# Biased attention: the ones column of V set on GpSimd, and a planner that counts TensorE at half clock in the prologue

## The chip, the cores and the metric

The kernel runs on one core of a Trainium2 chip. The metric is the time of one execution on the device, in microseconds; the figure of a kernel is the median of several executions. The core has engines that run side by side, each with its own queue worked off in order: TensorE (PE, matrix products and transposes), VectorE (DVE), ScalarE (ACT, here the exponentials), GpSimd (POOL) and SyncE (SP). Loads and stores are DMAs that are issued from the queues of SP, ACT and POOL. Engines wait for each other by semaphores.

## The reference

```python
scale = 1.0 / np.sqrt(head_dim)
scores = scale * np.matmul(q, k.transpose(0, 1, 3, 2))
scores = scores + bias                      # one bias, 1024 x 1024, for all heads
scores_max = np.max(scores, axis=-1, keepdims=True)
attn = np.exp(scores - scores_max) / (np.sum(np.exp(scores - scores_max), axis=-1, keepdims=True) + 1e-8)
return np.matmul(attn, v).astype(np.float32)
```

q, k and v are float32 of 4 batches x 8 heads x 1024 x 64, so 32 heads, which the kernel takes as 16 pairs.

## The kernel before

**Arithmetic.** The kernel writes exp(scale*qk + bias) as exp(scale*qk) * exp(bias). The scores are kept transposed, keys on the partitions. One "bank" is 128 keys x 512 queries of one head; a pair has 32 banks (2 halves of the queries, 8 key chunks, 2 heads), and there are 512 in all. For each bank:

- TensorE forms kT by qT into PSUM (`s_fill`, L125). Three banks make one "slot"; two slots fit in PSUM. Slot g is called S g below; slots 0 and 1 hold one and two banks.
- ScalarE takes the exponential of a slot at once into bf16 tiles E (`s_exp`, L130).
- VectorE multiplies two banks at a time by the exponential of the transposed bias (`mul_pair`, L148).
- TensorE multiplies E by V, which has a 65th column of ones, so that the row sums come out with the product (`av_bank`, L160). After 8 key chunks VectorE takes the reciprocal of the sum (L170) and scales the result (L171) into an output tile; SP stores one head at a time (L174).

The bias is transposed once on TensorE (`b_fill`, L138) and exponentiated by ScalarE (`b_exp`, L143) into eb, in four tiles: (0,0), (0,4), (1,0), (1,4), the first number the half of the queries, the second the first of four key chunks. A multiply needs the tile of its half and chunk.

Q and K of a pair are transposed in four "pieces" (`transpose_pe`, L88): K and Q, each in two halves. Every piece goes through one of two PSUM buffers, xa and xb, and VectorE copies it out (K: a plain copy, L101; Q: a multiply with a mask that keeps the two heads apart, L97). The av products use the same two buffers, and give one back when it has been evacuated. When the second Q piece of a pair has been copied, GpSimd is told to load q and k of the pair after the next two and V of the pair after the next.

**The prologue** is written out by hand: SP and ACT load the first halves of Q and K of pair 0 as float32; VectorE clears and fills the constants (L183 to L200), among them the ones column of all of V, `vall[:, :, :, D:D1]`, 256 elements in each of 128 partitions, 65 elements apart; GpSimd makes the identity and then issues, in this order, kr and qr of pair 0 (second halves), the first half of the bias (btraw), V of pair 0 (two loads, L80), K and Q of pair 1 (L74, L75), the second half of the bias (L203), V of pair 1, K and Q of pair 2. The first V load has to come after the ones column. VectorE casts the two heads of Q to bf16 (L221), TensorE transposes them (L224), VectorE copies them out (L225), and the first two slots run.

**The planner** sets everything after that. From L239 on, Python simulates the engines while it emits the program: it keeps the times t_act, t_pe and t_dve in nanoseconds, and at each step emits what can start first: ScalarE's next exponential, VectorE's next item (copies and evacuations before multiplies), or what `pe_pick` chooses for TensorE. TensorE's choices are the next fill of a slot or of a bias tile (`pe_fill`), the next piece (`pe_piece`) and the next av bank (`pe_av`). A piece or av bank is taken only if it ends before a limit, which is set by when the next fill is ready and when it has to be done for ScalarE not to wait. The planner's costs are constants (L239 and L240: a bank's matmul 216, an av bank 170, a piece 350, an exponential 45 + 427 for each bank, a multiply 600); the clock starts at T0; and a few times are fixed: `bias_at` and `raw_at` say when the loads of the bias and of pairs 0, 1 and 2 are taken to have landed. These costs decide only the order of the instructions in each queue. On the chip, semaphores decide when they run.

Order of the fills from slot 2 on: S2, S3, S4, S5, S6, bias tile (0,0), S7, bias tile (0,4), S8, S9, S10, bias tile (1,0), S11, bias tile (1,4), S12, and then slots alone.

Of the kernel before, what the change touches and what calls it, by code (L numbers as in the profile page):

```python
# [15 lines left out]
def kernel(  # L16
# [15 lines left out]
    nc = tc.nc  # L32
    B, H, S, D = q.shape
    P = 128
    NCH = S // P
    D1 = D + 1
# [25 lines left out]
    vall = consts.tile([P, 2 * NP, NCH, D1], BF)  # L62
# [15 lines left out]
    def load_v(pr):  # L78
        for t in range(2):
            nc.gpsimd.dma_start(out=vall[:, 2 * pr + t, :, :D], in_=vf[pr, :, t])  # L80
# [38 lines left out]
    def s_fill(g):  # L119
        ps = ps_s.tile([P, 3, HQ], F32, tag="s", name="ps")  # L120
        open_ps[("S", g)] = ps
        for j, b in enumerate(slots[g]):
            pr, h, qh, kc = banks[b]
            qT, kT = trs[(pr, 0)], trs[(pr, 1)]
            nc.tensor.matmul(ps[:, j, :], kT[:, kc, :], qT[:, h, qh * HQ:(qh + 1) * HQ],  # L125
                             start=True, stop=True)
# [5 lines left out]
    def b_fill(qh, k0):  # L132

        ps = ps_s.tile([P, 3, 2 * HQ], BF, tag="s", name="pb").rearrange("p b (j q) -> p (b j) q", j=2)
        open_ps[("B", qh, k0)] = ps
        for j in range(4):
            for i in range(QC):
                nc.tensor.transpose(ps[:, j, i * P:(i + 1) * P],  # L138
                                    btraw[:, qh * QC + i, :].rearrange("p (kp kc) -> p kc kp", kc=NCH)[:, k0 + j, :],
                                    ident[:])  # L140
# [36 lines left out]
    with tc.manual_schedule():  # L177
# [18 lines left out]
        for t in range(2):  # L196
            nc.vector.memset(qT0[t * D:(t + 1) * D, 1 - t, :HQ], 0.0)
            for u in range(2):
                nc.vector.memset(mask[t * D:(t + 1) * D, u, :], 1.0 if t == u else 0.0)
        nc.vector.memset(vall[:, :, :, D:D1], 1.0)  # L200
        load_v(0)
        load_qk(1)
        nc.gpsimd.dma_start(out=btraw[:, QC:, :], in_=bf_[:, QC:, :])  # L203
# [35 lines left out]

        EXP, EXP0, QK, AV, TP = 427, 45, 216, 170, 350
        MUL, COPYQ, COPYK, EVAC, SEM = 600, 650, 420, 620, 80
        order = [("S", g) for g in range(2, NS)]
        for at, x in ((5, (0, 0)), (7, (0, 4)), (11, (1, 0)), (13, (1, 4))):
            order.insert(at, ("B",) + x)
        NO = len(order)
        T0 = 7500.0
        t_act, t_pe, t_dve = T0 + 700, T0, T0 + 500
        filled = []  # L250
        act_end = []
        x_free = {"xa": T0 + 500, "xb": T0}
        x_unit = {}
# [3 lines left out]
        for pr in range(1, NP):  # L257
            pieces += [(pr, 1, 0), (pr, 0, 0), (pr, 1, 1), (pr, 0, 1)]
        piece_end = {(0, 1, 0): T0, (0, 0, 0): T0}
        eb_at = {}  # L260
        exp_at = {0: T0, 1: T0 + 700, 2: T0 + 700}
        mul_at = {}
# [9 lines left out]
        def unit_of(b):  # L272
            return banks[b][:3]

        dve_q = []

        def cost_act(i):
            item = order[i]
            return EXP0 + EXP * (len(slots[item[1]]) if item[0] == "S" else 4)

        def act_end_of(i):
            if i < 0:
                return T0
            if i < len(act_end):
                return act_end[i]
            return max(t_act, filled[i] + SEM if i < len(filled) else 0) + sum(
                cost_act(j) for j in range(len(act_end), i + 1))

        def pe_fill():
            i = len(filled)  # L290
            if i >= NO or i - 2 >= len(act_end):
                return None
            ready = act_end_of(i - 2) + SEM
            item = order[i]
            if item[0] == "S":
                for b in slots[item[1]]:
                    pr, h, qh, kc = banks[b]
                    for key in ((pr, 1, kc // QC), (pr, 0, qh)):
                        if key not in piece_end:
                            return None  # L300
                        ready = max(ready, piece_end[key] + SEM)
                cost = QK * len(slots[item[1]])
            else:
                ready = max(ready, bias_at[item[1]])
                cost = 2 * TP + 250

            def emit(t):
                if item[0] == "S":
                    s_fill(item[1])
                else:  # L310
                    b_fill(item[1], item[2])
                filled.append(t + cost)
            return ready, cost, emit

        def pe_piece():
            if not pieces:
                return None
            pr, which, half = pieces[0]
            if pr not in raw_at or pr not in raws:
                return None  # L320
            i = min(len(filled), NO - 1)
            while order[i][0] != "S":
                i -= 1
            at = slots[order[i][1]][0]
            if at < (pr - 2) * 32 + 8:
                return None

            left = NCH - av_next % NCH
            busy = x_unit.get(unit_of(av_order[av_next])) if av_next % NCH else None
            tags = sorted((x_free[x], x) for x in x_free if x != busy)  # L330
            if busy and left < 4 and at < pr * 32 - 16:
                return None
            if not busy and av_next and at < pr * 32 - 16 and tags[0][0] + SEM < t_pe and len(tags) > 1 and tags[1][0] > t_pe:
                return None
            free, tag = tags[0]
            ready = max(free + SEM, raw_at[pr][1 - which])

            def emit(t):
                pieces.pop(0)
                copy = transpose_pe(pr, which, half, tag)  # L340
                cost = COPYK if which else COPYQ
                x_free[tag] = 1e12

                def run(t2):
                    copy()
                    x_free[tag] = t2 + cost
                    piece_end[(pr, which, half)] = t2 + cost
                    if which == 0 and half == 1:
                        if pr + 3 < NP:
                            load_qk(pr + 3)  # L350
                            raw_at[pr + 3] = (t2 + 7000, t2 + 7000)
                        if pr + 2 < NP:
                            load_v(pr + 2)
                dve_q.append((t + TP + SEM, 0, cost, run))
            return ready, TP, emit

        def pe_av():
# [23 lines left out]
                    dve_q.append((t + AV + SEM, 1, EVAC, run))  # L381
            return ready, AV, emit

        def pe_pick():
            f = pe_fill()
            best = None
            i = len(filled)
            if f and f[0] <= t_pe:
                return (max(t_pe, f[0]),) + f[1:]
            limit = 1e12  # L390
            if f:
                limit = max(f[0], act_end_of(i - 1) - f[1] - 100)
            elif i < NO:
                limit = max(act_end_of(i - 2) + SEM, act_end_of(i - 1) - 750)
            for c in (pe_piece(), pe_av()):
                if c is None:
                    continue
                start = max(t_pe, c[0])
                if start + c[1] > limit:
                    continue  # L400
                if best is None or start < best[0]:
                    best = (start,) + c[1:]
            if f and (best is None or f[0] <= best[0]):
                best = (max(t_pe, f[0]),) + f[1:]
            return best
# [19 lines left out]
        def act_pick():  # L425
            i = len(act_end)
            if i >= len(filled):
                return None
            return max(t_act, filled[i] + SEM), cost_act(i), i

        while len(act_end) < NO or av_next < NB or dve_q:
            c = []
            a, d, p = act_pick(), dve_pick(), pe_pick()
            if a:
                c.append((a[0], 0))
            if d:
                c.append((max(t_dve, d[0]), 1))
            if p:
                c.append((p[0], 2))
            t, who = min(c)  # L440
            if who == 0:
                i = a[2]
                item = order[i]
                t_act = t + a[1]
                act_end.append(t_act)
                if item[0] == "S":
                    s_exp(item[1])
                    for b in slots[item[1]]:
                        exp_at[b] = t_act
                else:  # L450
                    b_exp(item[1], item[2])
                    for kc in range(4):
                        eb_at[(item[1], item[2] + kc)] = t_act
            elif who == 1:
                if d in dve_q:
                    dve_q.remove(d)
                t_dve = t + d[2]
                d[3](t)
            else:
                t_pe = t + p[1]  # L460
                p[2](t)


# [28 lines left out]
```

## Time and profile before

| | us |
|---|---|
| median of 4 executions | 254.51 (254.13 to 254.57) |
| the profiled execution | 254.13 |
| its span | 252.4 |
| ScalarE busy | 239.0 (95%) |
| TensorE busy | 232.4 (92%) |
| VectorE busy | 226.0 (90%) |
| GpSimd busy | 52.6 (21%) |
| exponentials, L130 | 172 instructions, 230.1 |
| multiplies, L148 | 256 instructions, 163.5 |

The span reaches from the first to the last thing that the profiler saw; the execution's own time is 1.73 us longer. Lines of a timeline give start and duration in us, engine, line, operation, what is written and read, how often in a row, and in square brackets the idle time before and what ended it. Lines of the table of groups end with busy us, the mean ns of one, and the idle time of the engine before them. "ps" is the PSUM of the scores, "px" that of the pieces, "po" that of the av products. A score matmul of 512 columns takes 0.45 us of TensorE in the prologue (five from 7.24 us on in 2.24) and 0.27 later (three from 9.98 us on in 0.82).

### The profile page before, as it was taken

The page shows a single profiled execution, that of the slowest core. Times are in us where ns is not written, and L with a number is a line of the kernel's source. Part 1 is how long each engine was busy: PE and PEld are TensorE (multiplying, and loading weights), DVE is VectorE, ACT ScalarE, POOL GpSimd, SP SyncE. Part 2 cuts the span into 40 slices and gives each one's busy share as a digit, 9 for nine tenths or more (in the row PEclk, how much of TensorE's full clock was granted, in tenths as well). Part 3 has the DMA queues.
Part 4 walks back from the last instruction along what each step waited for, and adds up shares of the span by engine and source line. Part 5 has one row for each costly group of instructions (what it writes and reads, how often), then busy time and mean ns, then how long its engine had stood idle before and what let it go on. Part 6 is the DMA issues. An engine that isn't in the chain of part 4 may idle for free.

```text
span 252.4 us, 7265 instructions
## 1 busy us (share of the span) xinstructions
PE 232.4 (92%) x3142; PEld 141.3 (56%) x3142; DVE 226.0 (90%) x461; ACT 239.0 (95%) x180; POOL 52.6 (21%) x72
## 2 busy tenths in 40 slices
PE   6869999999999999999999999999999999999982
PEld 2346655565565566565555566565555655555651
DVE  6219899999999999999999999999999999999994
ACT  3799999999999999999999999999999999999970
POOL 6743222422310513013042205034000000000000
PEclk9999999999999999999999999999999999999999
DMA  7999979979291589439186904939020201111112
GB/s 145 184 221 183 189 92 158 110 129 99 68 144 44 104 66 152 62 71 139 44 137 48 187 7 92 121 84 167 5 84 3 83 2 44 44 43 44 47 38 83
DMA packets 47743, 23.79 MB, mean 94 GB/s; under 512 B 34400, under 2 KB 43360, under 8 KB 47456
## 3 DMA queue, kind: packets, MB, share of 16 engines
q0 software_dynamic: 42272, 14.42, 52.8%
q1 hardware_dynamic: 5296, 8.78, 9.5%
q8 instruction: 24, 0.39, 0.7%
q10 hardware_dynamic: 144, 0.13, 0.1%
q14 instruction: 7, 0.06, 0.1%
HBM read 29.36 MB, written 8.39 MB: 150 GB/s over the span
## 4 chain that ended last, share of the span: by engine, by line
PE 44%; ACT 41%; DVE 10%; issue 2%; DMA 1%; ACTq 0%
ACT E L130 38%; PE ps L125 31%; PE po L160 8%; DVE E L148 6%; PE px L88 5%; ACT eb L143 3%; DVE oall L171 1%; DMA q0f<-in_q_dram 1%; DVE qT L97 1%; DVE rs L170 1%; ACTq L130 0%; DVE qT L225 0%; PE px L224 0%; DVE qr L221 0%; DVE kT L101 0%
## 5 line engine op out<-in xcount | busy, mean ns | idle before, releaser
L130 ACT ACTIVATE E<-ps 128x1536 bf16<-128x1536 f32 (+2 forms) x172 | 230.1, 1666 | 2.9 <-PE ps L125 2.9
L148 DVE TENSOR_TENSOR E<-E,eb 128x1024 bf16<-128x1024 bf16 x256 | 163.5, 682 | 7.4 <-ACT eb L143 7.3
L125 PE MATMUL ps<-qT,kT 128*128 128x512 bf16 x512 | 139.2, 380 | 9.3 <-ACT E L130 4.6
L160 PEld LDWEIGHTS <-E 128*128 128x128 bf16 x2048 | 84.4, 97 | 40.1 <-DVE E L148 2.5
L160 PE MATMUL po<-vall,E 128*128 128x65 bf16 x2048 | 96.3, 194 | 2.2 <-DVE E L148 1.3
L125 PEld LDWEIGHTS <-kT 128*128 128x128 bf16 x512 | 45.4, 97 | 42.4 <-issue 10.9
L74 POOL DMA_DIRECT2D kr<-in_k_dram x15 | 10.5, 699 | 97.4 <-PE px L88 94.9
L80 POOL DMA_DIRECT2D vall<-in_v_dram x32 | 28.1, 882 | 7.4 <-DMA btraw<-in_bias_dram 4.0
L171 DVE TENSOR_TENSOR oall<-po,rs 128x256 f32<-128x256 f32 x64 | 27.1, 424 | 2.4 <-DVE rs L170 0.3
L97 DVE TENSOR_TENSOR qT<-px,mask 128x1024 bf16<-128x1024 bf16 x31 | 21.3, 688 | 1.7 <-PE px L88 0.8
L101 DVE COPY kT<-px 128x512 bf16<-128x512 bf16 x31 | 13.1, 423 | 5.0 <-PE px L88 4.2
L170 DVE RECIPROCAL rs<-po 128x4 f32<-128x4 f32 x64 | 11.3, 176 | 3.5 <-PE po L160 3.1
L75 POOL DMA_DIRECT2D qr<-in_q_dram x15 | 10.7, 716 | 14.8 <-PE px L88 14.0
L88 PE MATMUL px<-ident,kr 128*64 128x128 bf16 x248 | 12.8, 225 | 0.2
L88 PE MATMUL px<-ident,qr 128*64 128x128 bf16 x248 | 12.8, 224 | 0.1
L88 PEld LDWEIGHTS <-kr 128*64 128x64 bf16 x248 | 7.9, 109 | 8.6 <-issue 5.5
L88 PEld LDWEIGHTS <-qr 128*64 128x64 bf16 x248 | 8.0, 109 | 7.6 <-issue 7.0
L143 ACT ACTIVATE eb<-pb 128x2048 bf16<-128x2048 bf16 x4 | 7.5, 1880 | 0.0
L138 PE MATMUL pb<-ident,btraw 128*128 128x128 bf16 x64 | 4.6, 224 | 1.9 <-ACT eb L143 1.0
L138 PEld LDWEIGHTS <-btraw 128*128 128x128 bf16 x64 | 4.6, 146 | 2.7 <-issue 2.4
L209 PE MATMUL wm<-zeros 128*128 128x512 bf16 x6 | 2.7, 630 | 1.2 <-DVE zeros L184 1.2
L185 ACT ACT_TABLE_LOAD x1 | 1.3, 1283 | 1.2 <-PEq L476 1.2
(27 smaller groups left out, 12.9 us busy)
## 6 DMA issues: line engine op xcount, KB each, us to landing
out_dram<-oall SPq DMA_DIRECT2D x32, 256.0 KB, 2.4
vall<-in_v_dram POOLq DMA_DIRECT2D x32, 128.0 KB, 6.1
kr<-in_k_dram POOLq DMA_DIRECT2D x15, 256.0 KB, 3.6
qr<-in_q_dram POOLq DMA_DIRECT2D x15, 256.0 KB, 5.3
btraw<-in_bias_dram POOLq DMA_DIRECT2D x2, 1024.0 KB, 10.7
k0f<-in_k_dram SPq DMA_DIRECT2D x2, 128.0 KB, 3.5
q0f<-in_q_dram ACTq DMA_DIRECT2D x1, 128.0 KB, 2.8
q0f<-in_q_dram SPq DMA_DIRECT2D x1, 128.0 KB, 2.7
```

Source lines behind the costliest of these rows:

```text
L75: nc.gpsimd.dma_start(out=qr.rearrange("p t c d -> p t (c d)"), in_=qf[pr])
L80: nc.gpsimd.dma_start(out=vall[:, 2 * pr + t, :, :D], in_=vf[pr, :, t])
L88: nc.tensor.transpose(px[t * D:(t + 1) * D, c, :], src[:, t, half * QC + c, :], ident[:])
L97: nc.vector.tensor_tensor(dst[:, :, half * HQ:(half + 1) * HQ], px.rearrange("p c q -> p (c q)").unsqueeze(1).to_broadcast([P, 2, HQ]), ma ...
L101: nc.vector.tensor_copy(dst[:, half * QC:(half + 1) * QC, :], px[:])
L125: nc.tensor.matmul(ps[:, j, :], kT[:, kc, :], qT[:, h, qh * HQ:(qh + 1) * HQ], start=True, stop=True)
L130: nc.scalar.activation(e_at(slots[g][0], n), open_ps.pop(("S", g))[:, :n, :], ACTF.Exp, scale=scale)
L143: nc.scalar.activation(eb[:, qh, k0:k0 + 4, :], open_ps.pop(("B", qh, k0))[:, :4, :], ACTF.Exp)
L148: nc.vector.tensor_tensor(e, e, eb[:, qh, kc:kc + 1, :].to_broadcast([P, n, HQ]), op=ALU.mult)
L160: nc.tensor.matmul(acc[:, i, :], e[:, 0, i * P:(i + 1) * P], vall[:, 2 * pr + h, kc, :], start=(kc == 0 and i == 0), stop=(kc == NCH - 1), ...
L170: nc.vector.reciprocal(rs[:], acc[:, :, D:D1])
L171: nc.vector.tensor_tensor(oall[:, qh * QC:(qh + 1) * QC, :], acc[:, :, :D], rs[:].to_broadcast([P, QC, D]), op=ALU.mult)
```

## The change

The diff has two parts. The memset of V's ones column is issued by GpSimd instead of VectorE; it stands at the same place in the program, after the first bias load and before the first V load. And the planner gets a time, COLD, before which everything on TensorE counts double; T0 is set from 7500 to 6700; and if nothing at all can be chosen, TensorE's limit is left aside for one choice. `bias_at` and `raw_at` stay as they are.

```diff
-        nc.vector.memset(vall[:, :, :, D:D1], 1.0)
+        nc.gpsimd.memset(vall[:, :, :, D:D1], 1.0)
...
+        COLD = 10500
...
-        T0 = 7500.0
+        T0 = 6700.0
...
+        def pe_cost(t, c):
+            return c * 2 if t < COLD else c
...
-                filled.append(t + cost)
+                filled.append(t + pe_cost(t, cost))
...
-                dve_q.append((t + TP + SEM, 0, cost, run))
+                dve_q.append((t + pe_cost(t, TP) + SEM, 0, cost, run))
...
-        def pe_pick():
+        def pe_pick(force=False):
...
-                limit = max(f[0], act_end_of(i - 1) - f[1] - 100)
+                limit = max(f[0], act_end_of(i - 1) - pe_cost(t_pe, f[1]) - 100)
...
-                if start + c[1] > limit:
+                if start + pe_cost(start, c[1]) > limit and not force:
...
             if p:
                 c.append((p[0], 2))
+            if not c:
+                p = pe_pick(force=True)
+                c.append((p[0], 2))
...
-                t_pe = t + p[1]
+                t_pe = t + pe_cost(t, p[1])
```

## The prediction

> **What bounds the kernel now.** I read the page's table of groups first, then the chain that ended last, then the waits of VectorE, then the timeline at three places: the prologue, the stretch from 16 to 31 us, the end. Columns of the groups: busy us, mean ns of one | idle before.
>
> ```profile
> span 252.4 us, 7265 instructions
> PE 44%; ACT 41%; DVE 10%; issue 2%; DMA 1%; ACTq 0%
> ...
> L130 ACT ACTIVATE E<-ps 128x1536 bf16<-128x1536 f32 (+2 forms) x172 | 230.1, 1666 | 2.9 <-PE ps L125 2.9
> L148 DVE TENSOR_TENSOR E<-E,eb 128x1024 bf16<-128x1024 bf16 x256 | 163.5, 682 | 7.4 <-ACT eb L143 7.3
> ```
>
> ScalarE's exponentials idle 2.9 us in all, and all of it lies before 9.52 us. From there ScalarE is full to its last exponential. But it does not set the end: VectorE does.
>
> ```profile
> 236.63 8.03 ACT L130 ACTIVATE E<-ps 128x1536 bf16<-128x1536 f32 x6
> ...
> 244.38 3.09 DVE L148 TENSOR_TENSOR E<-E,eb 128x1024 bf16<-128x1024 bf16 x5
> ...
> 248.63 0.42 DVE L171 TENSOR_TENSOR oall<-po,rs 128x256 f32<-128x256 f32 x1
> ```
>
> The last exponential ends at 236.63 + 8.03 = 244.66; VectorE then still owes five multiplies (to 247.47) and two evacuations (to 249.05), and the output's landing closes the span at 252.4. The waits of VectorE after 18.2 us name TensorE (3.1 + 2.0 + 0.8 us, for evacuations and transposed tiles) and never an exponential of L130: it runs behind ScalarE for 230 us. So two things move the end: when VectorE's stream of multiplies is let loose, and how much VectorE work stands behind that point. Where it is let loose:
>
> ```profile
> 16.24 1.88 ACT L143 ACTIVATE eb<-pb 128x2048 bf16<-128x2048 bf16 x1
> 18.15 1.90 DVE L148 TENSOR_TENSOR E<-E,eb 128x1024 bf16<-128x1024 bf16 x3 [7.26 <-ACT eb L143]
> ...
> 25.16 1.88 ACT L143 ACTIVATE eb<-pb 128x2048 bf16<-128x2048 bf16 x1
> 26.28 0.18 DVE L170 RECIPROCAL rs<-po 128x4 f32<-128x4 f32 x1 [1.10 <-PE po L160]
> ...
> 27.07 1.90 DVE L148 TENSOR_TENSOR E<-E,eb 128x1024 bf16<-128x1024 bf16 x3
> ```
>
> VectorE starts multiplying when the first exponentiated bias tile is out (16.24 + 1.88 = 18.12) and is stopped once more, until the third one is (25.16 + 1.88 = 27.04): the multiply at 27.07 needs it, and VectorE had idled 1.10 us before 26.28. Work saved before 25.2 us is swallowed there. What counts is ScalarE's clock at 27.04 and the VectorE work left after it.
>
> **Part 1: the memset moves from VectorE to GpSimd.** The prologue:
>
> ```profile
> 2.98 0.60 POOL L195 DMA_DIRECT2D btraw<-in_bias_dram  x1
> 4.31 0.49 DVE L221 CAST qr<-q0f 128x256 bf16<-128x256 f32 x1 [0.89 <-DMA q0f<-in_q_dram]
> 4.42 0.27 DVE L200 MEMSET vall<- 128x256 bf16 x1
> 4.72 0.28 DVE L221 CAST qr<-q0f 128x256 bf16<-128x256 f32 x1
> 4.86 0.83 PE L224 MATMUL px<-ident,qr 128*64 128x128 bf16 x8 [0.23 <-DVE qr L221]
> 4.98 1.75 POOL L80 DMA_DIRECT2D vall<-in_v_dram  x2 [1.40 <-DVE qr L221]
> 5.54 0.88 DVE L225 COPY qT<-px 64x512 bf16<-64x512 bf16 x2 [0.53 <-PE px L224]
> 6.44 0.39 DVE L213 CAST kr<-k0f 128x256 bf16<-128x256 f32 x1
> 9.52 5.48 ACT L130 ACTIVATE E<-ps 128x1536 bf16<-128x1536 f32 x4 [0.18 <-PE ps L125]
> ```
>
> The chain to 9.52 runs: q0f landed (3.56), the two casts (end 5.00), eight transposes, two qT copies, a cast of K, four transposes, five cold matmuls (0.45 us each), with 0.02 to 0.05 us between links. Anything taken off the casts arrives at 9.52 in full; the next floor is far, since K's second half lands at 5.68 and its cast starts at 6.44.
> Removed: 0.27 us of memset that lies between the casts. The first cast takes 0.49 over it, the second 0.28 alone. Without it: 4.31 + 0.28 + 0.28 = 4.87 instead of 5.00, so 0.13 us, and the first four transposes can start 0.2 earlier, which hides in the second four. I take **-0.14 us**. Upper bound: the memset waits for nothing, VectorE was free at 3.42, yet both it and the cast began only at 4.3 to 4.4. If that unexplained 0.9 us belongs to the memset, the casts run at 3.58 and 3.90, but TensorE is busy with K's transposes from 4.20 to about 4.32; eight transposes behind them end near 4.32 + 0.44 + 0.31 = 5.07 instead of 5.51: **-0.44 us**.
> Added on GpSimd: a memset of 128x256. Nearest rows: 128x1 takes 0.10, 128x128 takes 0.20, so 0.82 ns an element and 0.31 us for 256; doubled for the stride of 65, 0.6 us. It starts at 2.98 + 0.60 = 3.58 and is done by 3.9 to 4.2, under the 1.40 us in which GpSimd waits now: cost nothing. Behind it the queue (two vall loads, kr, qr, the second btraw, two vall) is issued some 0.9 us earlier, seven loads. These gain nothing: the first btraw load lands at 11.71 whatever follows, and those behind it land one by one at 12.77, 13.77, 14.69 and 15.97. The kr load of pair 2 at 12.00 waits for that 11.71.
> Against it: the vall issues (0.88 us each) now run from about 4.0 to 5.7, over the casts. By the row, the K cast at 6.44 lies inside a vall issue (5.86 to 6.73) and takes 0.39 against 0.28: 0.11 each, so the gain of 0.14 would become a loss of 0.08. By the Trainium skill (page "SBUF — State Buffer", section "Who interferes with whom") a VectorE cast from SBUF to SBUF in a 2-port mode and GpSimd, which writes the load's descriptors, exclude each other for a whole instruction: the first cast would wait for the issue that began at 4.0, to about 4.9, and the sum would turn to +0.5 or more. The row disagrees (the K cast ended 6.83, 0.1 us after that issue), so I keep the row, mostly unblocked.
>
> **Part 2: the emission model.** It sets only the order in each queue. I walked it by hand. Before: S2 7580, K pieces (0) 8228, Q piece (0) 8578, S3 9158, S4 9806, exponential of S3 9886. After: S2 6780 at doubled cost (to 8076). The K piece would end at 8776 against a limit of 8732: refused, so only the new forced choice takes it, at 8076 (to 8776). Q's piece would end 9476, past S3's ready time 9356: S3 goes first (to 10652), then S4 (10652), then Q's piece at 11300. The model's ScalarE from then on is 846 ns later than before (S5 at 12138 against 11292; the trace has it at 12.36). TensorE's real order becomes K piece, S3, S4, Q piece, S5. Cost: S3's last bank waits for the kT copy anyway (10.34 in the trace); the Q piece falls at 11.83, its copy ends by 13.0, S6 needs it at 13.70. Nothing. The loads that hang on that copy (kr, qr of pair 3, vall of pair 2) are held by an earlier load's landing at 13.77 already.
> The fixed landing times of the model do not move, so relative to its ScalarE they are 846 earlier. At S7 the K piece of pair 1 (fixed 17200) ends 17550, under the limit 18065: before, it would have missed it. So it moves ahead of the second bias transpose, and its copy ahead of the first multiply. Really: S7 ends at 17.2, transposes to 17.45, copy 17.5 to 17.92, before 18.12; K landed at 14.69. So 0.42 us goes into idle time, but ahead of 25.2, where it is swallowed.
> The next move stays: K's first piece of pair 2 comes after the fifth multiply-accumulate of the odd head (model 26068), its copy (0.42) ahead of the multiply at 27.07 instead of after four of them. Behind S11 and two av banks TensorE gets there near 26.7, since its av banks come earlier by the 0.4 saved; copy 26.95 to 27.37. The multiply is late by 0.30, the 0.42 is done: **-0.12 us**. Ends: TensorE 0.3 earlier, -0.42; 0.3 later, +0.18. Past this point my walk finds the same VectorE order up to the evacuation of bank 30, 181 ns ahead in the model.
>
> **Sum.** -0.14 - 0.12 = -0.26 us, taken as -0.3 with the small hidden parts. On the profiled execution: span 252.4 to 252.1, its time 254.13 (1.73 around the span) to 253.8. The median of the runs stands 0.38 above that execution, so I predict **254.2**. 0.2% of 254.51 is 0.51 us, about what a measurement can tell here: the likeliest outcome is inside it.
>
> **Rivals.**
> A, likeliest, 0.45: as summed, 254.2; its own range 253.8 to 254.7.
> B, 0.28: the 0.9 us hole in VectorE before 4.31 is the memset's. For: the memset had no wait to serve. Against: the cast is stamped before it, so the hole may be a common one. -0.44 - 0.12: 253.95.
> C, 0.17, the other side: the vall issues stall the casts as the page says. Place: between 4.0 and 5.7. Price: the first cast waits to 4.9 and so ends the second at 5.5, or at 6.0 if that waits for the second issue (to 5.75): +0.5 to +1.0 at 9.52, less 0.12: 254.9 to 255.4. It decides for slower once the casts end 0.63 us later than now, at 5.63.
> D, 0.10: the change does not do what it says: VectorE's hole stays, the pair 2 copy just holds the multiply by its own length: 254.5.
>
> Faster: most of B (0.23) and a sixth of A: 0.30. Slower: two thirds of C and a little of A and D, where a later flip of av and transposes costs VectorE half a microsecond: 0.20. Same: 0.50. The range goes from B's good end, 253.6, to C's middle, 255.1.
>
> **What would show it.** Right: casts ending near 4.9, ScalarE full from about 9.4, one kT copy before the first multiply, a kT copy between 26.3 and 27.4, five multiplies still owed after the last exponential. B: casts at 3.6 and 3.9. C: casts longer than 0.6 us while vall loads are issued. Wrong: ScalarE idle after 9.5 us, or VectorE's waits for TensorE well over the present 5.9 us.

## The result, and the profile after

The changed kernel takes **253.66 us** (median of 37 executions, 252.62 to 254.20), the kernel before 254.57 beside it (58 executions): ratio 0.9963, interval 0.9952 to 0.9973. That is 0.37% faster: 0.94 us by the ratio, 0.91 by the medians. The time lies inside the stated range (253.6 to 255.1), outside the likeliest case's own range (253.8 to 254.7), and on the side of "faster", which had 0.30 against 0.50 for "same". It is inside by 0.06 us, and by luck: the lower end of the range was set for rival B, which this change does not bring about, and most of the gain comes from a stretch to which the prediction gave nothing.

The page of the changed kernel answers to the first lines shown of before: the span is 0.6 us shorter, ScalarE's exponentials are as long as they were, and VectorE's multiplies have lost their one long wait for the exponentiated bias (7.4 us of idle is now 0.2).

```profile
span 251.8 us, 7268 instructions
PE 43%; ACT 34%; DVE 19%; issue 1%; ACTq 0%
...
L130 ACT ACTIVATE E<-ps 128x1536 bf16<-128x1536 f32 (+2 forms) x172 | 230.1, 1681 | 3.3 <-PE ps L125 3.3
L148 DVE TENSOR_TENSOR E<-E,eb 128x1024 bf16<-128x1024 bf16 x256 | 163.5, 682 | 0.2
```

That lost wait is no gain by itself. The waits of VectorE show where it went: to the K copy (L101) that now stands ahead of the first multiply and waits for TensorE instead. It was 4.2 us in ten waits before, and one wait of 4.7 us has come in.

```profile
DVE kT L101 <- PE px L88: 9.8, 11, 4.7
DVE qT L97 <- PE px L88: 2.8, 6, 1.8
DVE rs L170 <- PE po L160: 2.2, 9, 0.5
```

The timeline of the prologue, changed kernel (start and duration in us):

```profile
3.46 1.71 DVE L221 CAST qr<-q0f 128x256 bf16<-128x256 f32 x2
3.53 1.28 POOL L200 MEMSET vall<- 128x256 bf16 x1
5.02 0.83 PE L224 MATMUL px<-ident,qr 128*64 128x128 bf16 x8 [0.59 <-DVE qr L221]
5.11 1.75 POOL L80 DMA_DIRECT2D vall<-in_v_dram  x2 [0.30 <-POOL vall L200]
6.60 0.36 DVE L213 CAST kr<-k0f 128x256 bf16<-128x256 f32 x1
9.72 4.17 ACT L130 ACTIVATE E<-ps 128x1536 bf16<-128x1536 f32 x3 [0.26 <-PE ps L125]
```

The casts begin 0.85 us earlier than before (3.46 for 4.31), but they end at 5.17, 0.17 later than before, because the memset on GpSimd takes 1.28 us and runs right beside them. The exponential of S2 starts at 9.72; it was 9.52. The head is worse, not better.

The timeline in the middle and at the end, changed kernel:

```profile
17.83 0.42 DVE L101 COPY kT<-px 128x512 bf16<-128x512 bf16 x1 [4.72 <-PE px L88]
...
25.39 1.88 ACT L143 ACTIVATE eb<-pb 128x2048 bf16<-128x2048 bf16 x1
27.01 0.42 DVE L101 COPY kT<-px 128x512 bf16<-128x512 bf16 x1 [0.72 <-PE px L88]
27.35 2.49 DVE L148 TENSOR_TENSOR E<-E,eb 128x1024 bf16<-128x1024 bf16 x4
...
235.51 9.38 ACT L130 ACTIVATE E<-ps 128x1536 bf16<-128x1536 f32 x7
...
244.41 2.48 DVE L148 TENSOR_TENSOR E<-E,eb 128x1024 bf16<-128x1024 bf16 x4
...
248.05 0.42 DVE L171 TENSOR_TENSOR oall<-po,rs 128x256 f32<-128x256 f32 x1
```

Both early K copies are where the prediction put them: one ahead of the first multiply, one from 27.01 to 27.43 (26.3 to 27.4 was foreseen). At the end, though, VectorE runs four multiplies in its last group, not the five that the prediction named as a sign of being right. From the end of the last exponential (235.51 + 9.38 = 244.89) to the end of the last evacuation (248.05 + 0.42 = 248.47) it takes 3.58 us; before, 244.65 to 249.05, 4.40.

**How the traces are compared below.** The head differs between executions of one kernel (last section), so a whole time of one trace says little. I cut each trace at E, the end of the exponential of the third bias tile: the point at which the prediction saw VectorE's stream let loose for good. Before: E = 25.16 + 1.88 = 27.04, last evacuation 249.05, so 222.01 us from E to the end. After: E = 25.39 + 1.88 = 27.27, last evacuation 248.47, so 221.20. From E on the change wins 0.81 us; in front of E it loses 0.23 in this pair. The sum, 0.58, is the pair's difference in the last evacuation (249.05 - 248.47); the spans differ by 0.6.

### The profile page after: what moved, and what is told of

It reads as the page before. It is cut to its first block, busy times and chain, and to the rows that moved or that the text cites. A ratio compares the mean times of both kernels' runs of the same rounds, so it can differ in the third digit from the quotient of the medians.

```text
span 251.8 us, 7268 instructions
## 1 busy us (share of the span) xinstructions
PE 232.5 (92%) x3142; PEld 141.1 (56%) x3142; DVE 226.9 (90%) x460; ACT 239.0 (95%) x180; POOL 53.9 (21%) x73
## 4 chain that ended last, share of the span: by engine, by line
PE 43%; ACT 34%; DVE 19%; issue 1%; ACTq 0%
ACT E L130 32%; PE ps L125 28%; DVE E L148 13%; PE po L160 9%; PE px L88 5%; ACT eb L143 3%; DVE oall L171 3%; DVE rs L170 1%; DVE qT L97 1%; DVE qr L221 1%; DVE mask L199 1%; DVE kT L101 0%; ACTq L130 0%; DVE qT L225 0%; PE px L224 0%
## 5 line engine op out<-in xcount | busy, mean ns | idle before, releaser
L160 PE MATMUL po<-vall,E 128*128 128x65 bf16 x2048 | 97.3, 194 | 2.8 <-DVE E L148 1.3
L101 DVE COPY kT<-px 128x512 bf16<-128x512 bf16 x31 | 13.1, 423 | 10.7 <-PE px L88 9.8
```

The lines of the kernel that those rows point to most:

```text
L101: nc.vector.tensor_copy(dst[:, half * QC:(half + 1) * QC, :], px[:])
L160: nc.tensor.matmul(acc[:, i, :], e[:, 0, i * P:(i + 1) * P], vall[:, 2 * pr + h, kc, :], start=(kc == 0 and i == 0), stop=(kc == NCH - 1), ...
```

## The experiments

The theory after the result: the planner's order (part 2) brings all of the gain, behind E, and the memset on GpSimd (part 1) costs a little in the head. The rivals: that the memset's departure from VectorE brings it (rival B's hole), and that within part 2 it is the half clock (the Q piece behind S3 and S4 on TensorE) and not the earlier K copies.

**p1_gpsimd: part 1 alone**, on the kernel before.

```diff
-        nc.vector.memset(vall[:, :, :, D:D1], 1.0)
+        nc.gpsimd.memset(vall[:, :, :, D:D1], 1.0)
```

> The memset alone is moved to GpSimd; the planner is that of before, so TensorE, ScalarE and all of VectorE but the memset keep their order. Theory 1 (the gain of the whole change lies in the order, and the memset's move costs time): the casts again end about 0.2 us late under the memset on GpSimd, ScalarE is full from about 9.7 us, and the time is 0 to 0.3 us above before. Theory 2 (the memset's move gives the gain: VectorE relieved, V loads issued earlier): 0.6 to 0.9 us below before.

Measured: 254.63 us, ratio 1.0005 (0.9990 to 1.0019). From E to the end 222.02. The timeline of its prologue shows the same collision as the changed kernel's, so the memset alone makes it:

```profile
3.54 1.28 POOL L200 MEMSET vall<- 128x256 bf16 x1
3.70 1.47 DVE L221 CAST qr<-q0f 128x256 bf16<-128x256 f32 x2 [0.27 <-DMA q0f<-in_q_dram]
...
9.73 1.45 ACT L130 ACTIVATE E<-ps 128x1536 bf16<-128x1536 f32 x1 [0.26 <-PE ps L125]
```

Part 1 gains nothing that can be measured.

**p2_planner: part 2 alone**, on the changed kernel.

```diff
-        nc.gpsimd.memset(vall[:, :, :, D:D1], 1.0)
+        nc.vector.memset(vall[:, :, :, D:D1], 1.0)
```

> The new planner alone; the memset stays on VectorE. Theory 1: the prologue is that of before (ScalarE full from 9.5 us) and the order is that of after, so the time is 0 to 0.3 us below after, 0.9 to 1.2 below before. Theory 2: the time of before, within 0.2 us.

Measured: 253.57 us, ratio 0.9963 (0.9949 to 0.9978), the same ratio as the whole change. From E to the end 221.21. The gain is part 2's.

**p2_fixed_shift: part 2 without the relative shift of the fixed times.** The half clock and the new T0 stay; the times that the planner takes as fixed are moved later by the 846 ns by which its ScalarE is later, which puts VectorE's order back to that of before. The edit is made on p2_planner.

```diff
-        bias_at = [13500, 22000]
-        raw_at = {0: (6000, 7500), 1: (17200, 18300), 2: (26000, 28500)}
+        bias_at = [14346, 22846]
+        raw_at = {0: (6000, 7500), 1: (18046, 19146), 2: (26846, 29346)}
```

> The new planner with the memset on VectorE, and the fixed landing times of the bias and of pairs 1 and 2 moved later by the same 846 ns as the model's ScalarE; that puts VectorE back into the order of before, while TensorE keeps S3 and S4 ahead of Q's second piece. Theory 1a (the gain comes from the order of pieces, multiplies and evacuations after 17 us): the gain is gone, within 0.3 us of before. Theory 1b (it comes from the head of the model, the half clock and Q's piece behind S4): the time of the new planner alone.

Measured: 254.37 us, ratio 0.9998 (0.9977 to 1.0019). From E to the end 222.02. Half clock without the early K copies brings nothing.

**old_early: the early K copies without the half clock.** The kernel before, with only the landing times of pairs 1 and 2 846 ns earlier. VectorE's order is then exactly that of the changed kernel; TensorE's differs in the Q piece alone. The edit is made on the kernel before.

```diff
-        raw_at = {0: (6000, 7500), 1: (17200, 18300), 2: (26000, 28500)}
+        raw_at = {0: (6000, 7500), 1: (16354, 17454), 2: (25154, 27654)}
```

> The kernel of before with one edit: the fixed landing times of pairs 1 and 2 are 846 ns earlier. No half clock, T0 and memset of before. VectorE then gets exactly the order of after (all its copies, multiplies and evacuations), TensorE that of after but for Q's second piece, which stays ahead of S3. If the early pieces are the whole of the gain: from the end of the third bias exponential to VectorE's last evacuation 221.2 us as in after (222.0 in before), and the time of the new planner alone, 0.996 of before. If the half clock has a part of its own: 222.0 and no gain, or something between.

Measured: from E to the end 221.22, as with the whole of part 2. The ratio, 0.9983 (0.9960 to 1.0005), is too wide to decide by itself (12 executions, 252.51 to 254.47); the stage decides. Four landing times in the planner's table thus do what the whole of part 2 does.

**p2_pair2_late: the pair 1 copy early, the pair 2 copy late.** The edit is made on p2_planner.

```diff
-        raw_at = {0: (6000, 7500), 1: (17200, 18300), 2: (26000, 28500)}
+        raw_at = {0: (6000, 7500), 1: (17200, 18300), 2: (26900, 29400)}
```

> The new planner with the memset on VectorE, and the landing times of pair 2 alone 900 ns later. The K copy of pair 1 still comes ahead of the first multiply, but no copy of pair 2 ahead of the third bias exponential. If, as predicted, work saved before that exponential is swallowed by the wait for it: 222.0 us from its end to VectorE's last evacuation (0.3 either way for the different order after it). If the early copy of pair 1 is worth something by itself: 221.4 to 221.7.

Measured: one execution, 255.04 us; from E to the end 222.02. The timeline of VectorE:

```profile
18.46 0.42 DVE L101 COPY kT<-px 128x512 bf16<-128x512 bf16 x1 [4.26 <-PE px L88]
...
27.93 1.30 DVE L148 TENSOR_TENSOR E<-E,eb 128x1024 bf16<-128x1024 bf16 x2 [1.02 <-ACT eb L143]
```

The 0.42 us of the first copy are done early, and VectorE then idles 1.02 us for E. So the pair 1 copy is swallowed, as predicted, and the gain hangs on the pair 2 copy's place and on the order that the planner chooses behind it. This run also shows what becomes of a lag. At the multiply of bank 148 its VectorE is 0.47 us behind the kernel before (times from E, at points where both have done the same work); from bank 204 on it has that kernel's order, and there it is never more than 0.13 behind, and from bank 264 on 0.01. The waits for TensorE wipe the difference out.

**p2_m400: the landing times of pairs 1 and 2 400 ns earlier than in p2_planner.** The planner then takes another order in the middle of the run. The edit is made on p2_planner.

```diff
-        raw_at = {0: (6000, 7500), 1: (17200, 18300), 2: (26000, 28500)}
+        raw_at = {0: (6000, 7500), 1: (16800, 17900), 2: (25600, 28100)}
```

> The new planner with the memset on VectorE, landing times of pairs 1 and 2 400 ns earlier. The same early copies (pair 1 ahead of the first multiply, pair 2 ahead of the multiply that waits for the third bias exponential), but a later order that differs from after's in 88 of 382 VectorE items. If the 0.54 us that after saved beyond 30 us follows from VectorE's lead there: 221.2 us again from the third bias exponential to the end, within 0.15. If it is the luck of one order: some other figure, 221.2 to 222.0, with 0.27 saved up to the multiply of bank 24 in any case.

Measured: one execution, 252.51 us; from E to the end 221.22. It was to part two readings: that the time won at the pair 2 copy is kept to the end, or that the planner's order of the last stretch happens to be a better one. By its end time alone it does not, because its last 150 VectorE items of 382 are those of the changed kernel, while p2_pair2_late shares its last 222 with the kernel before. Every order that was run ends in one of two tails, 4.40 us or 3.6 us behind the last exponential.

**split: the memset in two pieces on VectorE**, under the new planner. Only V of pairs 0 and 1 is loaded in the prologue, so only their 32 elements (4 heads x 8 key chunks) are set ahead of the first V load; the other 224 go behind the second slot's exponential, where VectorE waits anyway. The edit is made on p2_planner.

```diff
-        nc.vector.memset(vall[:, :, :, D:D1], 1.0)
+        nc.vector.memset(vall[:, :4, :, D:D1], 1.0)
...
         for g in range(1, 2):
             s_fill(g)
             s_exp(g)
+        nc.vector.memset(vall[:, 4:, :, D:D1], 1.0)
```

> The new planner; the ones of pairs 0 and 1 alone are set where VectorE set all of them (32 elements a partition instead of 256), the other 224 on VectorE after the last copy of the prologue, where it idles from 7.6 to 9.9 us. If the hole of VectorE ahead of the casts belongs to the memset (1.27 us for 256, so 0.16 for 32): casts at 3.6 and 3.9, ScalarE full from 9.1, 0.3 to 0.5 us below the new planner alone. If the hole has another cause: casts at 4.3 again, at most 0.15 below it.

Measured: **252.22 us**, ratio 0.9927 (0.9901 to 0.9952): faster than both kernels. From E to the end 221.22; S2's exponential starts at 8.11, against 8.69 in p2_planner, both with TensorE at full clock by 5 us. The timeline of VectorE:

```profile
3.52 0.29 DVE L221 CAST qr<-q0f 128x256 bf16<-128x256 f32 x1
3.61 0.09 DVE L200 MEMSET vall<- 128x32 bf16 x1
3.90 0.29 DVE L221 CAST qr<-q0f 128x256 bf16<-128x256 f32 x1
...
6.65 0.29 DVE L218 COPY kT<-px 128x256 bf16<-128x256 bf16 x1 [0.40 <-PE px L217]
7.71 0.24 DVE L239 MEMSET vall<- 128x224 bf16 x1 [0.77 <-issue]
```

The hole has gone with the 224 elements. Where they stand now a hole has opened ahead of them, 0.77 us with no releaser but "issue". The hole is the memset's, and the row of 0.24 us is only its end. Its going reaches S2, which depends on the K cast, in two ways. The timelines of p2_planner, first, and of split:

```profile
4.99 1.75 POOL L80 DMA_DIRECT2D vall<-in_v_dram  x2 [1.41 <-DVE qr L221]
6.22 0.62 DVE L213 CAST kr<-k0f 128x256 bf16<-128x256 f32 x1
```

```profile
3.99 1.75 POOL L80 DMA_DIRECT2D vall<-in_v_dram  x2 [0.41 <-DVE qr L221]
5.96 0.29 DVE L213 CAST kr<-k0f 128x256 bf16<-128x256 f32 x1
```

Behind the earlier casts of Q the K cast begins 0.26 us earlier (5.96 for 6.22). And it takes 0.33 less: in p2_planner it ends 0.10 us behind the issue of the V loads (6.84 and 6.74), in split the V loads, too, are issued 1.00 us earlier, their issue is over at 5.74, and the cast takes its 0.29.

The median is 1.35 us below p2_planner's, where 0.3 to 0.5 had been expected: a miss. The fastest executions of the two are 0.63 apart (251.87 and 252.50), the two traces 0.36 (252.14 and 252.50). In split's lowest group lie 5 of 8 executions, in p2_planner's 4 of 22; that may be the rest of the distance between the medians. Of the 0.58 us that S2 comes earlier, 0.39 arrive at E (25.80 for 26.19). The chain that ended last, of split, names what is next: the second half of the bias lands at 22.64, and the transposes of the third bias tile wait for it. ScalarE, which waits for them, ends the tile at 25.80.

```profile
7.13 15.51 DMA btraw<-in_bias_dram
22.69 1.21 PE pb L138 x16
23.92 1.88 ACT eb L143
25.80 1.34 ACT E L130
```

**split_flat: what of GpSimd's 1.28 us is the stride.** As split, and GpSimd sets an extra tile of 256 contiguous elements, which nothing reads. The edit is made on split.

```diff
+        flat = consts.tile([P, 2 * NP * NCH], BF)
+        nc.gpsimd.memset(flat[:], 1.0)
```

> As the kernel with the ones split, and GpSimd in addition sets a contiguous, unused tile of 128x256 where after sets the ones. If GpSimd's memset was slow (1.28 us) because of the stride: 0.3 us here, and VectorE's casts end near 3.9 to 4.2 as with the split alone. If any memset on GpSimd takes that long beside the casts (they exclude each other): 1 us or more, casts ending near 5.

Measured: one execution, 253.29 us; from E to the end 221.22. GpSimd's row and the cast beside it:

```profile
3.50 0.32 DVE L223 CAST qr<-q0f 128x256 bf16<-128x256 f32 x1
3.54 0.52 POOL L202 MEMSET flat<- 128x256 bf16 x1
```

Contiguous, the same number of elements takes 0.52 us at most where the strided ones took 1.28, and the cast that began 0.04 us earlier is hardly longer (0.32 for 0.29). At most, because that cast runs beside the memset until 3.82, and the memset may have waited for it; then 0.24 us would be its own. The later head of this execution (S2 at 9.34) goes with a clock that got full only at 9.68.

**g_early: the memset on GpSimd, but where no cast is.** The changed kernel with the memset ahead of GpSimd's first load.

```diff
+        nc.gpsimd.memset(vall[:, :, :, D:D1], 1.0)
         nc.gpsimd.dma_start(out=kr0[:, :, QC:, :].rearrange("p t c d -> p t (c d)"), in_=kf[0][:, :, QC * D:])
...
-        nc.gpsimd.memset(vall[:, :, :, D:D1], 1.0)
```

> As after, but GpSimd sets the ones before its first load, so from 1.3 us on, with no cast of VectorE near it; its loads are issued some 1.3 us later. If the 1.28 us is the price of the stride: 1.28 us again, the casts free (3.5 and 3.9), V's loads issued near 4.9, the prologue 0.4 us or more shorter than after's; the time 0.3 to 0.6 us below after. If it was the casts that stretched it: 0.3 to 0.5 us here, as for the contiguous tile.

Measured: 253.45 us, ratio 0.9959 (0.9942 to 0.9976). The timeline:

```profile
1.25 1.23 POOL L193 MEMSET vall<- 128x256 bf16 x1
3.46 0.87 DVE L221 CAST qr<-q0f 128x256 bf16<-128x256 f32 x2
```

With no cast beside it the memset still takes 1.23 us, and with no memset beside them the two casts take 0.87 where they took 1.71. S2's exponential starts at 8.19. But K of pair 2 lands at 25.41, only 0.28 us ahead of E (0.74 in split), and its transposes wait 0.42 us for it. So the multiply that needs the third bias tile starts 0.56 us behind E instead of 0.08, ScalarE idles 0.24 us at 27.03, and E to the end becomes 221.56: of what the head wins, 0.36 us (221.56 - 221.20) is given back. The first three loads are issued 0.64 us later than in the changed kernel, those of V 0.94 earlier; whether that order makes pair 2 late, one trace does not show. The median is 0.21 us below the changed kernel's, where 0.3 to 0.6 had been expected: a miss.

**split_old: the split memset under the old planner.** The edit is made on the kernel before.

```diff
-        nc.vector.memset(vall[:, :, :, D:D1], 1.0)
+        nc.vector.memset(vall[:, :4, :, D:D1], 1.0)
...
+        nc.vector.memset(vall[:, 4:, :, D:D1], 1.0)
```

> The split of the ones with the planner of before. If the two gains add: casts at 3.5 and 3.9 and 222.0 us from the third bias exponential to the end, 0.4 to 0.6 us below before (0.998) and 0.8 above the split with the new planner.

Measured: 253.06 us, ratio 0.9957 (0.9941 to 0.9974). S2 at 8.03, E to the end 222.02. Head and order are worth about 0.4% each (0.9957 and 0.9963), and split, with both, has 0.9927: within the intervals they add. Against the kernel before the gain is 1.1 us by the ratio, where 0.4 to 0.6 had been expected: a miss. Against split, 0.84 as expected.

**split_warm: one more matmul on zeros** between the transposes of Q and the first scores, to hold TensorE's clock. The edit is made on split.

```diff
         c_b = q_first(1, "xb")
+        nc.tensor.matmul(wm[:, 0, :], zeros[:, :P], zeros[:], start=True, stop=True)
```

> The split with the new planner, and one more unused matmul of 512 columns on zeros, where TensorE waits for the copies of Q (4.9 to 5.5 us). In the traces so far TensorE's clock got full at 4.5, 4.7, 4.9, 9.3, 9.7, 9.9, 11.9, 12.5 and 13.2 us, and the executions of one kernel lie in groups up to 2 us apart. If the gaps of TensorE before 6 us decide that: full clock near 5 us in most executions, executions closer together, median near 251.9. If not: the spread and the median of the split, 252.2.

Measured: 252.25 us, ratio 0.9920 (0.9896 to 0.9944); five of six executions lie between 252.23 and 252.28, one at 253.32. The median is split's, not the 251.9 I expected: a miss. Split's eight spread from 251.87 to 253.49, so the spread looks narrower, but six executions do not settle it.

The stages of the traces, from the start and end times of their instructions:

| | S2's exponential | E | last evacuation | E to the end | clock full at |
|---|---|---|---|---|---|
| before | 9.52 | 27.04 | 249.05 | 222.01 | 9.27 |
| after | 9.72 | 27.27 | 248.47 | 221.20 | 9.91 |
| p1_gpsimd | 9.73 | 28.29 | 250.31 | 222.02 | 12.46 |
| p2_planner | 8.69 | 26.19 | 247.41 | 221.21 | 4.54 |
| p2_fixed_shift | 9.60 | 27.72 | 249.74 | 222.02 | 11.87 |
| old_early | 8.69 | 26.20 | 247.41 | 221.22 | 4.68 |
| p2_pair2_late | 9.78 | 27.90 | 249.93 | 222.02 | 13.24 |
| p2_m400 | 8.69 | 26.19 | 247.41 | 221.22 | 4.47 |
| split | 8.11 | 25.80 | 247.02 | 221.22 | 4.94 |
| split_flat | 9.34 | 26.96 | 248.18 | 221.22 | 9.68 |
| g_early | 8.19 | 25.69 | 247.25 | 221.56 | 5.91 |
| split_old | 8.03 | 25.81 | 247.83 | 222.02 | 4.08 |
| split_warm | 8.42 | 25.93 | 247.15 | 221.22 | 5.98 |

## Why the prediction was right and wrong

**What bounds the kernel: right.** ScalarE sets E and the last exponential (217.6 us lie between them in every trace but g_early's), VectorE sets the end, and only its order behind E and the head could move it.

**The pair 1 copy, swallowed: right.** p2_pair2_late keeps it and has the 222.02 of before.

**The pair 2 copy, -0.12: the mechanism right.** The prediction let the copy hold the next multiply by 0.30 us (27.37 for 27.07) and save 0.42. (It also put the copy behind the odd head's fifth multiply-accumulate; its model time, 26068, is that of bank 5, the odd head's third.) In the trace TensorE was earlier than I had put it against E: the multiply starts 0.08 us behind E (27.35 against 27.27), where it was 0.03 before, so the copy costs 0.05, and 0.37 would be left. It does not all arrive, because the fourth bias tile stops VectorE once more, which the prediction overlooked. The kernel before first, then the changed one:

```profile
28.27 1.88 ACT L143 ACTIVATE eb<-pb 128x2048 bf16<-128x2048 bf16 x1
30.45 1.28 DVE L148 TENSOR_TENSOR E<-E,eb 128x1024 bf16<-128x1024 bf16 x2
34.60 0.68 DVE L148 TENSOR_TENSOR E<-E,eb 128x1024 bf16<-128x1024 bf16 x1
```

```profile
28.50 1.88 ACT L143 ACTIVATE eb<-pb 128x2048 bf16<-128x2048 bf16 x1
30.42 1.29 DVE L148 TENSOR_TENSOR E<-E,eb 128x1024 bf16<-128x1024 bf16 x2
34.77 0.68 DVE L148 TENSOR_TENSOR E<-E,eb 128x1024 bf16<-128x1024 bf16 x1
```

The multiply of bank 24 needs the fourth tile. It stood 0.30 us behind the tile before (30.45 and 30.15) and now stands 0.04 behind (30.42 and 30.38): **-0.26** is about all that can be won there, and the stated end of -0.42 was out of reach. Of this lead, 0.06 us is left at the multiply of bank 34 (34.60 - 27.04 = 7.56 before, 34.77 - 27.27 = 7.50 after), with one order of VectorE in both kernels from bank 24 to there.

**"Past this point my walk finds the same VectorE order up to the evacuation of bank 30": true, but the step that failed.** The prediction took that as the end of the matter and carried nothing beyond it. At that evacuation (34.06 before, 34.21 after) the change is 0.08 us ahead, near the -0.12; at the end it is **0.81** ahead. The two orders part again eleven items later, near 40 us; of 382 VectorE items only 201 stand in the same place. So 0.73 of the 0.81 us arise where the prediction had nothing. It shows at the end as one multiply less in the last group (2.48 us for four, 3.09 for five) and a start of that group that is 0.48 us ahead of the last exponential's end, where it was 0.27: 0.61 + 0.21 = 0.82.

What sets it is where VectorE last stands waiting for TensorE. The timeline of the kernel before:

```profile
242.07 0.18 DVE L170 RECIPROCAL rs<-po 128x4 f32<-128x4 f32 x1 [0.26 <-PE po L160]
```

Until 242.07 VectorE is tied to TensorE there, and what is left behind that point takes 6.98 us. After the change the reciprocal of that place does not wait, and 6.96 us are left behind it:

```profile
241.51 0.17 DVE L170 RECIPROCAL rs<-po 128x4 f32<-128x4 f32 x1
```

The last wait of over 0.1 us ahead of it is one of 0.14 us, at 223.50. Shown is that part 2's order has this tail, that the four landing times of old_early are enough for it, and that the lead of 0.26 us at 30 us is not what is carried there: it is down to 0.06 by 35 us, and p2_pair2_late loses a lag of 0.47 us on its way. What counts is the order that the planner chooses behind it. Not shown is which of its later choices makes the better tail, or whether a still better one exists.

**Part 1, -0.14: wrong in sign.** Compared where the clock was likewise not yet full, S2's exponential starts at 9.72 and 9.73 with the memset on GpSimd and at 9.60 on VectorE (p2_fixed_shift): **+0.12**. That is two traces against one, and a fourth trace does not fit by itself: p2_pair2_late, also with the memset on VectorE and the clock not full, has 9.78, but its K cast waited 0.31 us for its load. Two steps failed. The memset on GpSimd was put at 0.31 to 0.6 us from contiguous rows; it took 1.28 (1.23 alone). And "under the 1.40 us in which GpSimd waits now: cost nothing" looked at GpSimd's queue alone, not at what VectorE does in that time. The casts had to wait for the memset: as single instructions the first one ends at 4.97, 0.16 us behind the memset's end (4.81).

The prediction had weighed the page "SBUF — State Buffer" of the Trainium skill, section "Who interferes with whom" (a VectorE cast in a 2-port mode and GpSimd exclude each other for a whole instruction), against the load issues alone, and let one row overrule it. For the memset the rule held to 0.16 us, though the first cast's row begins 0.07 us ahead of the memset's. For the loads the row was misread: that the K cast ended 0.1 us behind an issue was no sign against waiting for it. In nine traces the K cast begins 0.27 to 0.52 us before the end of a load's issue, and in all nine it ends 0.09 to 0.11 us behind that end, with durations from 0.36 to 0.62 us. But casts that were done before the last part of an issue kept their 0.29: split's at 5.96, begun 0.49 us before an end and done 0.19 before it, and split_old's at 4.16, done 0.48 before it. So it is not the whole issue that holds a cast, as the prediction applied the rule, but its last part. What GpSimd does in that part no trace shows.

So rival C had the right mechanism, and in this kernel it was the memset that the Q casts met. Its price was +0.12, not +0.5 to +1.0, since the memset began beside the casts and was over at 4.81.

**Rival B's hole: the premise right.** The 0.89 us ahead of 4.31 in the kernel before is the memset's. Split takes the hole away and S2 comes 0.58 us earlier (8.11 for 8.69), more than the bound of -0.44; 0.33 of it is the K cast that no longer meets an issue of the V loads, which the bound did not count. The change itself cannot have it: it moves the same stretch to the engine that the casts have to wait for.

**"Behind it the queue is issued some 0.9 us earlier": wrong.** The V loads are issued at 5.11 for 4.98, since the memset lasts to 4.81. Nor is the time of these issues without a price, as the prediction had it: the K cast ends 0.1 us behind them in both kernels, at 6.96 for 6.83, and this 0.13 is what arrives at S2.

**The Q piece behind S3 and S4, nothing: right.** old_early keeps it in its old place and has the same 221.22 us from E to the end.

**The sum.** Predicted -0.14 - 0.12 = -0.26; the traces give +0.12 - 0.81 = -0.69, the measured ratio -0.94. The 0.25 that is left between these two is no more than the half-width of the measured interval (0.0021 / 2 x 254.57 = 0.27 us), and I do not assign it. The fastest executions of the two kernels (253.28 and 252.62) are 0.66 apart, the slowest (255.28 and 254.20) 1.08. Part 1 had the wrong sign, and what more than made up for it was not in the sum.

## What to carry to other kernels

Where an order comes out of a planner, walk it to the end: nine tenths of this gain (0.73 of 0.81 us) lay behind the point at which the walk by hand stopped, in how much work the bounding engine still owed after its last wait. A lead in the middle of a run can be wiped out by waits for another engine. Before a small instruction is moved to an idle engine, ask how it reads or writes memory and who shares that access: 256 strided elements took 1.3 us on either engine, and the cheap answer was to set only the 32 that were needed and the rest in a wait. A hole ahead of an instruction with nothing to wait for may be the instruction itself.

## What the hardware showed unexpectedly

**A strided memset costs by the element, and its row hides it on VectorE.** 256 elements, 65 apart, in 128 partitions: GpSimd shows 1.23 and 1.28 us. VectorE shows a row of 0.27, but is free at 3.42 and ends the memset at 4.69: 1.27. In split, 32 elements end 0.28 us after 3.42, and 224 end 1.01 us after the copy before them (6.94 to 7.95), with 0.24 in the row. From the two pieces that is (1.01 - 0.28) / 192 = 3.8 ns an element, from 32 and 256 together (1.27 - 0.28) / 224 = 4.4, where a contiguous memset on GpSimd took 0.52 / 256 = 2.0 at most.

**A VectorE cast that meets the end of a load's issue on GpSimd ends just behind it.** It was 0.09 to 0.11 us behind the issue in nine traces and took up to 0.62 us for 0.29. So the time at which a load is issued can matter even where the time at which it lands does not.

**The moment at which TensorE's clock gets full moves the whole time by about 1 us.** It comes between 4.08 and 13.24 us in these traces, with the same work ahead of it in most. The groups of score matmuls in the prologue show the price, first in p2_planner (full at 4.54), then in p2_fixed_shift (full at 11.87):

```profile
7.12 1.25 PE L125 MATMUL ps<-qT,kT 128*128 128x512 bf16 x5
```

```profile
7.25 2.31 PE L125 MATMUL ps<-qT,kT 128*128 128x512 bf16 x5
```

The same five take 1.06 us more. With the first, S2's exponential starts at 8.69, with the second at 9.60. The executions of one kernel lie in groups accordingly (p2_planner: 252.5, 253.3 to 253.6, 254.0); that the groups are the clock's moments is seen only for the executions that have a trace (252.5 at 4.54, 4.47 and 4.68). This is why the stages were compared here and not whole traces.
